# The rows' scales reach all partitions through a small vector in DRAM and a repeating transfer, in place of a product of ones with a diagonal

## The chip, the cores and the metric

The kernel runs on one core of a Trainium2 chip. The metric is the device time of one execution in microseconds (us), here the median of several; lower is better. The engines of the core are named as in the profile: PE is TensorE (matrix products), PEld its loading of weights, DVE is VectorE, ACT ScalarE, POOL GpSimd, and SP is SyncE, which in this kernel issues nearly all transfers between DRAM and the on-chip memory, in the order of its queue. Each engine works through its own queue in order and waits on semaphores for the others.

## The reference

A decoder of two layers over 2048 rows of 1024 features: a gated retention layer (phase A) and a gated sliding-window attention layer (phase B). What matters here is the row scale, the reciprocal root mean square of a row, which multiplies the input of every projection:

```python
def rms(x):
    xf = x.astype(jnp.float32)
    return (xf * lax.rsqrt(jnp.mean(xf * xf, axis=-1, keepdims=True) + EPS)).astype(x.dtype)

def rmsnorm(x, g):
    return (rms(x) * g).astype(x.dtype)

def retention_layer(x, g_norm, w_in, w_out, sin, cos):
    proj = rmsnorm(x, g_norm) @ w_in
    q, k, v, gate = jnp.split(proj, ...)
    ...
    o = rms(retention(q, k, v)) * silu(gate)
    return x + o @ w_out

def swa_layer(x, g_norm, w_in, g_q, sinks, w_out, k_band, v_band, bias, mask):
    proj = rmsnorm(x, g_norm) @ w_in
    ...
    return x + (attention(q, k_band, v_band, bias, sinks) * silu(gate)) @ w_out
```

## The kernel before

The rows are worked on in four groups g of T = 512, with the features on the 128 partitions and the rows along the free axis. Products in float32 accuracy are made of three passes each, since both factors are split into a high and a low part (raw, whi and wlo for weights; ACT makes the high part at L125 and DVE the low part at L126).

Phase A has 16 units u, one for each group g and retention head h. A unit projects q and k (pp_a2qk and so on, with u in the name; the rotation of the result, L580 to L585, frees the PSUM banks), then v and the gate. From unit 4 on, v and the gate (tensors named a6v, a10v) are made by a Strassen scheme with seven products, p = 0 to 6. In parallel runs the retention of the unit before (names ending in _r: S is the state, Shi and Slo its parts, dl its increment, o the output, kt and ot transposes) and its output projection (pp_ao). Phase B has eight units (g, kv) with the attention.

The row scales have to reach all partitions, since the rows lie along the free axis, while the statistics give them as r, a tile of 128 x 4 with row 128 m + p at partition p, column m. This is done at seven places, in two functions, and the same way in both: DVE scales the unit matrix by each column of r, which gives four diagonal blocks (128 x 512); PE multiplies a matrix of ones with it (a float32 product, two passes), so that each of the 128 partitions gets the 512 scales; DVE copies the result from PSUM.

- stage_rows(g), for g = 1, 2, 3, prepares the inputs of the next group in DRAM, during the last units of the group before. Diagonal dgx (L313), product rpx (L315), copy rbx (L317). Then four rounds k follow: two loads xst (L323), their scaling by the gain ags and rbx on DVE (L327), four sums for the Strassen scheme (L331 to L334), two stores xn (L337) and four stores xS (L339). Six buffers (tag st) hold the round's tiles. Its scales r come from row_stats (POOL, L301). I call these three places sites 1, 2 and 3.
- scales(g), for g = 0 to 3, serves phase B. It loads the sums of squares (L169), adds them over the partitions (ssq, L172), makes r on POOL (L175), then the diagonal (L178), the product rp (L180) and the copy rb (L181). r itself is used early by the keys and values; rb is used first by the gates. It is called once at the end of phase A (L819) and by row_scales in phase B.

Both run beside other work. In phase A a list named behind holds such pieces as generators; step() advances the first of them by one yield at fixed points of a unit's projections. The function drive interleaves the projections of one unit with the retention of the one before. In phase B, at(i, ...) puts a call i steps ahead. The order in which the program is written does not set the queues by itself: the kernel is built under TileContext(schedule_with_timeline_sim=True), which orders each engine's queue by a modelled timeline.

## Time and profile before

| | |
|---|---|
| time, median of 3 runs | 2477.26 us (2474.19 to 2480.29) |
| the profiled execution | 2477.26 us, span 2475.5 us |
| granted TensorE clock | 0.993 |
| busy: PE, DVE, ACT, POOL | 98%, 66%, 43%, 9% |
| moved by transfers | 500 MB, 202 GB/s |

The span is what the profile shows of the execution, from its first instruction to its last; 1.76 us of the time lie around it. Starts in the timelines count from the span's start. A group's row gives the busy time, the mean time of one instruction, and how long its engine sat idle just before them; a row of the waits gives total, times and longest.

### The profile page before, as it was taken

The page shows a single profiled execution, that of the slowest core. Times are in us where ns is not written, and L with a number is a line of the kernel's source. Part 1 is how long each engine was busy: PE and PEld are TensorE (multiplying, and loading weights), DVE is VectorE, ACT ScalarE, POOL GpSimd, SP SyncE. Part 2 cuts the span into 40 slices and gives each one's busy share as a digit, 9 for nine tenths or more (in the row PEclk, how much of TensorE's full clock was granted, in tenths as well). Part 3 has the DMA queues.
Part 4 walks back from the last instruction along what each step waited for, and adds up shares of the span by engine and source line. Part 5 has one row for each costly group of instructions (what it writes and reads, how often), then busy time and mean ns, then how long its engine had stood idle before and what let it go on. Part 6 is the DMA issues. An engine that isn't in the chain of part 4 may idle for free.

```text
span 2475.5 us, 32133 instructions
## 1 busy us (share of the span) xinstructions
PE 2418.5 (98%) x11576; PEld 1965.9 (79%) x11576; DVE 1624.1 (66%) x2898; ACT 1055.0 (43%) x2028; POOL 234.6 (9%) x288
## 2 busy tenths in 40 slices
PE   8999999999999999999999999999999999999997
PEld 6888778887878888887788888887687787777776
DVE  5546665787778668588667765744656566566665
ACT  4333233543536455355455543433424334334332
POOL 0000000110001020001002000022101101102010
PEclk9999999999999999999999999999999999999998
DMA  8433843589786477498548843646554674655661
GB/s 297 141 116 128 285 136 115 187 310 322 228 285 218 129 255 265 134 309 296 160 153 292 290 128 94 207 149 220 192 204 147 231 239 136 211 201 184 201 216 69
DMA packets 178075, 499.97 MB, mean 202 GB/s; under 512 B 20363, under 2 KB 32956, under 8 KB 177916
## 3 DMA queue, kind: packets, MB, share of 16 engines
q1 hardware_dynamic: 177836, 497.66, 59.8%
q8 instruction: 91, 1.49, 0.2%
q14 instruction: 68, 0.56, 0.1%
q0 software_dynamic: 80, 0.26, 0.0%
HBM read 396.11 MB, written 104.88 MB: 202 GB/s over the span
## 4 chain that ended last, share of the span: by engine, by line
PE 54%; DVE 4%; DMA 3%; ACT 1%; SPq 0%; issue 0%; POOL 0%; ACTq 0%; DVEq 0%; POOLq 0%
PE o_t L1117 3%; PE pp_ao L146 2%; PE pp_ao L147 2%; PE pp_ao L148 2%; PE s_t L1068 2%; PE pp_bo L256 2%; PE pp_bo L255 2%; PE pp_bo L257 2%; PE pT_t L1099 1%; PE qtp_b L963 1%; DVE P_t L1071 1%; DMA wlo<-in_w_b 1%; PE ot_r L726 0%; PE o_r L698 0%; PE o_r L700 0%; PE o_r L699 0%
## 5 line engine op out<-in xcount | busy, mean ns | idle before, releaser
L146 PE MATMUL pp_ao<-ohi_r,whi_ao 128*128 128x512 f32 x512 | 198.8, 392 | 6.5 <-ACT whi_ao L125 5.5
L147 PE MATMUL pp_ao<-olo_r,whi_ao 128*128 128x512 f32 x512 | 199.6, 390 | 0.0
L148 PE MATMUL pp_ao<-ohi_r,wlo_ao 128*128 128x512 f32 x512 | 194.2, 390 | 0.9 <-DVE wlo_ao L126 0.9
L1071 DVE CUSTOM_DVE_ANT_0 P_t<-s_t,bias,nsnk 128x256 f32<-128x256 f32 (+1 forms) x256 | 115.1, 472 | 89.7 <-PE s_t L1068 80.1
L1081 ACT ACTIVATE P_t<-P_t,nm_t 128x128 f32<-128x128 f32 x256 | 100.4, 394 | 117.2 <-DVE P_t L1078 114.9
L766 DVE TENSOR_TENSOR x_r<-x_r,pp_ao 128x512 f32<-128x512 f32 x128 | 86.4, 683 | 63.7 <-PE pp_ao L148 63.4
L114 POOL TENSOR_SCALAR r_o_r<-sso_r,ep 128x1 f32<-128x1 f32 x48 | 34.8, 725 | 900.9 <-ACT jo_r L720 900.9
L146 PEld LDWEIGHTS pp_ao<-ohi_r,whi_ao 128*128 128x128 f32 x512 | 96.0, 188 | 27.7 <-ACT whi_ao L125 6.7
L795 ACT CAST Shi_r<-S 128x512 fp32r<-128x512 f32 x120 | 69.9, 618 | 112.3 <-PE o_r L700 74.0
L148 PEld LDWEIGHTS pp_ao<-ohi_r,wlo_ao 128*128 128x128 f32 x512 | 96.1, 188 | 21.6 <-DVE wlo_ao L126 1.6
L147 PEld LDWEIGHTS pp_ao<-olo_r,whi_ao 128*128 128x128 f32 x512 | 96.3, 188 | 19.7
L1068 PEld LDWEIGHTS s_t<-kst,qst_b 128*128 128x128 f32 x512 | 81.9, 193 | 30.5 <-DVE nm_t L1071 11.4
L1068 PE MATMUL s_t<-kst,qst_b 128*128 128x256 f32 (+1 forms) x512 | 97.6, 296 | 8.4 <-DVE nm_t L1071 8.2
L125 ACT CAST whi_ao<-raw_ao 128x1024 fp32r<-128x1024 f32 x64 | 67.1, 1049 | 90.0 <-DMA raw_ao<-in_wo_a 21.9
L796 DVE TENSOR_TENSOR Slo_r<-S,Shi_r 128x512 fp32r<-128x512 f32 x120 | 81.0, 704 | 34.0 <-ACT Shi_r L795 33.8
L126 DVE TENSOR_TENSOR wlo_ao<-raw_ao,whi_ao 128x1024 fp32r<-128x1024 f32 x64 | 78.2, 1222 | 33.5 <-ACT whi_ao L125 33.3
L713 DVE SCALAR_TENSOR_TENSOR S<-S,dl_r 128x512 f32<-128x512 f32 x112 | 74.3, 682 | 27.9 <-PE dl_r L692 27.8
L1102 ACT COPY pTs_t<-pT_t 128x512 f32<-128x512 f32 x64 | 37.3, 583 | 121.1 <-PE pT_t L1099 120.8
L256 PE MATMUL pp_bo<-olo_t,whi_bo 128*128 128x512 f32 x224 | 88.3, 394 | 0.0
L257 PE MATMUL pp_bo<-ohi_t,wlo_bo 128*128 128x512 f32 x224 | 88.2, 394 | 0.0
L255 PE MATMUL pp_bo<-ohi_t,whi_bo 128*128 128x512 f32 x224 | 85.5, 397 | 0.5 <-ACT ohi_t L1136 0.5
L964 ACT CAST qst_b<-qtp_b 128x512 fp32r<-128x512 f32 x64 | 37.4, 585 | 84.0 <-PE qtp_b L963 83.9
(1040 smaller groups left out, 7129.5 us busy)
## 6 DMA issues: line engine op xcount, KB each, us to landing
raw_ao<-in_wo_a SPq DMA_DIRECT2D x64, 512.0 KB, 4.1
b<-in_w_vg SPq DMA_DIRECT2D x64, 256.0 KB, 4.8
res<-xmid SPq DMA_DIRECT2D x28, 512.0 KB, 4.4
whi_bo<-wo SPq DMA_DIRECT2D x28, 512.0 KB, 3.9
wlo_bo<-wo SPq DMA_DIRECT2D x28, 512.0 KB, 4.8
x_r<-in_x_t SPq DMA_DIRECT2D x16, 512.0 KB, 6.4
xin<-in_x SPq DMA_DIRECT2D x16, 512.0 KB, 3.6
xmid<-x_r SPq DMA_DIRECT2D x16, 512.0 KB, 4.9
```

Of the source, the lines that this page charges most:

```text
L126: nc.vector.tensor_tensor(lo, raw, hi.bitcast(F32), op=ALU.subtract)
L146: nc.tensor.matmul(o, hi[:, kk, sl], xh, start=st, stop=False)
L147: nc.tensor.matmul(o, hi[:, kk, sl], xl, start=False, stop=False)
L148: nc.tensor.matmul(o, lo[:, kk, sl], xh, start=False, stop=sp)
L255: nc.tensor.matmul(o, hi[:, kk, sl], xh, start=s, stop=False)
L256: nc.tensor.matmul(o, hi[:, kk, sl], xl, start=False, stop=False)
L257: nc.tensor.matmul(o, lo[:, kk, sl], xh, start=False, stop=e)
L766: nc.vector.tensor_tensor(t, t, ps, op=ALU.add)
L796: nc.vector.tensor_tensor(lo, src[:, d, :], hi.bitcast(F32), op=ALU.subtract)
L1068: nc.tensor.matmul(o, q[:, h, :], kst[:, kv * 2 + hl, kb + b0 : kb + 2, :], start=hl == 0, stop=hl == 1)
L1071: nc.vector.tensor_tensor_reduce(out=pt[:, j, :w], in0=o, in1=bias[:, kv * GQ + h, b0 * P :], scale=-1.0, scalar=nsnk[:, kv * GQ + h : kv ...
L1081: nc.scalar.activation(pt[:, i, :P], pt[:, i, :P], AF.Exp, scale=-1.0, bias=nm[:, i : i + 1], accum_out=den[:, i : i + 1])
```

## The change

A new function, spread, writes r to a vector rd of 512 elements in DRAM (a transfer that writes single elements, since r has the rows of a block on the partitions), and returns a function that loads rd into all 128 partitions, 2 KB into each. The two transfers are issued on SP; the second waits for the landing of the first. The diagonals, the products and the copies go. scales becomes a generator: it yields after the load of the sums, after r, between the two transfers and at its end. scales(0) now stands in the list behind during the last but one unit, and row_scales takes its steps by at(1 to 4). stage_rows yields between the two transfers. The diagonal's buffers go as well (tag sta has one in place of two).

```diff
@@ -163,10 +163,16 @@
 
     scaled = {}
 
-    def scales(g, tiles, tag, rb):
-
-        acc, dg = tiles
+    def spread(r, name):
+
+        d = dram.tile([T], F32, name=f"rd_{name}")
+        nc.sync.dma_start(d.rearrange("(m p) -> p m", p=P), r)
+        return lambda rb: nc.sync.dma_start(rb, d.partition_broadcast(P))
+
+    def scales(g, acc, tag, rb):
+
         nc.sync.dma_start(acc, sqs[g])
+        yield
         ps = bank(f"ssq_{g}", tag)
         for m in range(MT):
             nc.tensor.matmul(ps[:, m : m + 1], acc[:, m * P : (m + 1) * P], ones[:, :1], start=True, stop=True)
@@ -174,12 +180,12 @@
         nc.vector.tensor_scalar(eps, ps[:, :MT], 1.0 / D, EPS, op0=ALU.mult, op1=ALU.add)
         nc.gpsimd.tensor_tensor(r, eps, neghalf[:, :MT], op=ALU.pow)
         nc.vector.tensor_scalar_mul(eps, eps, EPS)
-        for m in range(MT):
-            nc.vector.tensor_scalar_mul(dg[:, m * P : (m + 1) * P], ident, r[:, m : m + 1])
-        rp = bank(f"rp_{g}", tag)
-        nc.tensor.matmul(rp, ones, dg, start=True, stop=True)
-        nc.vector.tensor_copy(rb, rp)
         scaled[g] = r, eps, rb
+        yield
+        load = spread(r, f"b{g}")
+        yield
+        load(rb)
+        yield
 
     def out_proj(src, ohi, olo, evac, name):
         pre = []
@@ -308,14 +314,10 @@
             d = st["rows", g] = [dram.tile([P, 2, T], F32, name=f"xn{kp}_{g}") for kp in range(KT // 2)]
             ds = st["rsums", g] = {n: dram.tile([P, KT // 2, H], F32, name=f"x{n}_{g}") for n in SX}
             r = st["stats", g][1]
-            dg = stp(f"dgx_{g}")
-            for m in range(MT):
-                nc.vector.tensor_scalar_mul(dg[:, m * P : (m + 1) * P], ident, r[:, m : m + 1])
-            rp = bank(f"rpx_{g}")
-            nc.tensor.matmul(rp, ones, dg, start=True, stop=True)
+            load = spread(r, f"x{g}")
+            yield
             rb = small.tile([P, T], F32, tag="rb", bufs=1, name=f"rbx_{g}")
-            nc.vector.tensor_copy(rb, rp)
-            yield
+            load(rb)
             for k in range(KT // 2):
                 t = [stp(f"xst_{g}_{k}_{j}") for j in range(2)]
                 for j in range(2):
@@ -810,13 +812,14 @@
             if u + 1 in (8, 9, 10, 12, 13, 14):
                 behind.append(stage_b(todo[:9]))
                 del todo[:9]
+            if u + 1 == nu - 1:
+                behind.append(scales(0, short("acc_0"), "rr", small.tile([P, T], F32, tag="rb", bufs=1, name="rb_0")))
             drive(tc, main(u + 1), ret(u), 2 if u + 1 < PLAIN else 3, 0)
             for _ in itertools.islice(bias, 2 if u >= RH else 0):
                 pass
             if u < nu - 2:
                 for _ in out_a(u):
                     pass
-        scales(0, [short(f"stb_{i}") for i in range(2)], "rr", small.tile([P, T], F32, tag="rb", bufs=1, name="rb_0"))
         rows = load_xb(0)
 
         def beside():
@@ -1033,8 +1036,10 @@
 
         def row_scales(g):
             pool, tag = ((small, "rb"), (p1, "rb1"))[g % 2]
-            scales(g, [p1.tile([P, T], F32, tag="sta", bufs=2, name=f"st{i}_{g}") for i in range(2)], "f",
-                   pool.tile([P, T], F32, tag=tag, bufs=1, name=f"rb_{g}"))
+            work = scales(g, p1.tile([P, T], F32, tag="sta", bufs=1, name=f"acc_{g}"), "f",
+                          pool.tile([P, T], F32, tag=tag, bufs=1, name=f"rb_{g}"))
+            for i in range(4):
+                at(i + 1, next, work)
 
         def rows(g):
```

Line numbers grow by 2 or 3 behind the edit: the scaling is L329 now, the sums L333 to L336, the rotation L582 to L585, and the update of the state S, at L713 before, is L715. The scheduler orders the queues anew. Three places of DVE's queue follow; the numbers at the ends of names are the tiles' own.

DVE at site 1, ahead of the projections of unit 2 (xst_1_0_0: group 1, round 0, first tile; wlo_a2qk_11 is the last piece of the weights for q and k of unit 2). Before:

```order
L313 TENSOR_SCALAR dgx_1_1863<-ident_r_128,rx_1_1577 128x128 x4
L723 SCALAR_TENSOR_TENSOR gate_a1_0_1325<-o_r1_0_1508,r_o_r1_0_1523,gate_a1_0_1325 128x512
L126 TENSOR_TENSOR wlo_a2qk_11_1668<-raw_a2qk_11_1665,whi_a2qk_11_1667 128x1024
L126 TENSOR_TENSOR wlo_a2v_0_1794<-raw_a2v_0_1791,whi_a2v_0_1793 128x1024
L732 TENSOR_TENSOR olo_r1_1470<-ot_r1_0_1527,ohi_r1_1469 128x4x128
L713 SCALAR_TENSOR_TENSOR S32_1_1471<-S32_1_1471,dl_r1_1_0_1610 128x512
L713 SCALAR_TENSOR_TENSOR S32_1_1471<-S32_1_1471,dl_r1_1_1_1614 128x512
L796 TENSOR_TENSOR Slo_r1_1_1638<-S32_1_1471,Shi_r1_1_1637 128x512 x2
L723 SCALAR_TENSOR_TENSOR gate_a1_1_1327<-o_r1_1_1618,r_o_r1_1_1648,gate_a1_1_1327 128x512
L674 SCALAR_TENSOR_TENSOR klo_r1_1_1634<-kt_r1_1_1628,khi_r1_1_1633 128x512
```

And now:

```order
L725 SCALAR_TENSOR_TENSOR gate_a1_0_1325<-o_r1_0_1508,r_o_r1_0_1523,gate_a1_0_1325 128x512
L329 SCALAR_TENSOR_TENSOR xst_1_0_0_1897<-xst_1_0_0_1897,ags_122,rbx_1_1895 128x512
L329 SCALAR_TENSOR_TENSOR xst_1_0_1_1898<-xst_1_0_1_1898,ags_122,rbx_1_1895 128x512
L126 TENSOR_TENSOR wlo_a2qk_11_1668<-raw_a2qk_11_1665,whi_a2qk_11_1667 128x1024
L333 TENSOR_TENSOR xss_1_0_0_1934<-xst_1_0_0_1897,xst_1_0_1_1898 128x256
L335 TENSOR_TENSOR xss_1_0_1_1935<-xst_1_0_0_1897 128x256
L126 TENSOR_TENSOR wlo_a2v_0_1794<-raw_a2v_0_1791,whi_a2v_0_1793 128x1024
L334 TENSOR_TENSOR xss_1_0_0_1934<-xss_1_0_0_1934,xst_1_0_0_1897 128x256
L734 TENSOR_TENSOR olo_r1_1470<-ot_r1_0_1527,ohi_r1_1469 128x4x128
L715 SCALAR_TENSOR_TENSOR S32_1_1471<-S32_1_1471,dl_r1_1_0_1610 128x512
L329 SCALAR_TENSOR_TENSOR xst_1_1_0_1999<-xst_1_1_0_1999,ags_122,rbx_1_1895 128x512
L715 SCALAR_TENSOR_TENSOR S32_1_1471<-S32_1_1471,dl_r1_1_1_1614 128x512
```

In the diagonal's place, but behind the gate, stand the two scalings of round 0, which need the broadcast rbx; the weights' parts for unit 2 come behind them, and the scalings of round 1 stand among the updates of the state and ahead of the next gate. Rounds 2 and 3 follow in the same way, round 2 ahead of the rotation (L582) and round 3 ahead of its last part. Before, the first scaling stood behind all of these. In SP's queue the two transfers stand behind the second load of the weights for v; the stores of round 0 follow them, then the loads of round 1.

DVE at site 2, in the Strassen products p = 5 and 6 of unit 6 (wlo_a6v_60 and _61 are the weights of p = 6). Before:

```order
L313 TENSOR_SCALAR dgx_2_5583<-ident_r_128,rx_2_5445 128x128 x4
L126 TENSOR_TENSOR wlo_a6v_50_5560<-raw_a6v_50_5557,whi_a6v_50_5559 128x1024
L126 TENSOR_TENSOR wlo_a6v_51_5595<-raw_a6v_51_5592,whi_a6v_51_5594 128x1024
L431 TENSOR_TENSOR r_a6v_40_5547<-r_a6v_40_5547,pp_a6vb30_5450 128x512
L431 TENSOR_TENSOR r_a6v_41_5548<-r_a6v_41_5548,pp_a6vb31_5451 128x512
L317 COPY rbx_2_5590<-rpx_2_5588 128x512
L126 TENSOR_TENSOR wlo_a6v_60_5621<-raw_a6v_60_5618,whi_a6v_60_5620 128x1024
L327 SCALAR_TENSOR_TENSOR xst_2_0_0_5614<-xst_2_0_0_5614,ags_122,rbx_2_5590 128x512
L327 SCALAR_TENSOR_TENSOR xst_2_0_1_5615<-xst_2_0_1_5615,ags_122,rbx_2_5590 128x512
L651 TENSOR_TENSOR s_r6_5831<-sc_r6_5822,mask_164 128x512
L331 TENSOR_TENSOR xss_2_0_0_5638<-xst_2_0_0_5614,xst_2_0_1_5615 128x256
```

And now:

```order
L126 TENSOR_TENSOR wlo_a6v_50_5555<-raw_a6v_50_5552,whi_a6v_50_5554 128x1024
L126 TENSOR_TENSOR wlo_a6v_51_5583<-raw_a6v_51_5580,whi_a6v_51_5582 128x1024
L329 SCALAR_TENSOR_TENSOR xst_2_0_0_5604<-xst_2_0_0_5604,ags_122,rbx_2_5602 128x512
L329 SCALAR_TENSOR_TENSOR xst_2_0_1_5605<-xst_2_0_1_5605,ags_122,rbx_2_5602 128x512
L433 TENSOR_TENSOR r_a6v_40_5542<-r_a6v_40_5542,pp_a6vb30_5445 128x512
L433 TENSOR_TENSOR r_a6v_41_5543<-r_a6v_41_5543,pp_a6vb31_5446 128x512
L715 SCALAR_TENSOR_TENSOR S32_6_5470<-S32_6_5470,dl_r6_0_0_5840 128x512
L333 TENSOR_TENSOR xss_2_0_0_5628<-xst_2_0_0_5604,xst_2_0_1_5605 128x256
L335 TENSOR_TENSOR xss_2_0_1_5629<-xst_2_0_0_5604 128x256
L715 SCALAR_TENSOR_TENSOR S32_6_5470<-S32_6_5470,dl_r6_0_1_5844 128x512
L126 TENSOR_TENSOR wlo_a6v_60_5611<-raw_a6v_60_5608,whi_a6v_60_5610 128x1024
L653 TENSOR_TENSOR s_r6_5821<-sc_r6_5812,mask_164 128x512
```

The scalings stand ahead of the last additions (L433) and of wlo_a6v_60, and the updates of the state S, which stood much later, come ahead of it too. In PE's queue the six passes dl of this update, the first three of the output o and, further on, its last three were moved forward with them: the first use of wlo_a6v_60 is ten passes further back in the queue than before, that of wlo_a6v_61 fifteen, the product rpx taken off.

DVE at site 3, ahead of the rotation of unit 10. Before:

```order
L126 TENSOR_TENSOR wlo_a10qk_11_8643<-raw_a10qk_11_8640,whi_a10qk_11_8642 128x1024
L126 TENSOR_TENSOR wlo_a10v_00_8774<-raw_a10v_00_8771,whi_a10v_00_8773 128x1024
L713 SCALAR_TENSOR_TENSOR S32_9_8192<-S32_9_8192,dl_r9_1_0_8674 128x512
L713 SCALAR_TENSOR_TENSOR S32_9_8192<-S32_9_8192,dl_r9_1_1_8678 128x512
L796 TENSOR_TENSOR Slo_r9_1_8702<-S32_9_8192,Shi_r9_1_8701 128x512
L580 TENSOR_TENSOR q_a10_8558<-pp_a10qk_0_8560,cos_a8_6764 128x512
L581 TENSOR_TENSOR th_a10_0_1_8754<-pp_a10qk_0_8560,sin_a8_6765 128x512
L796 TENSOR_TENSOR Slo_r9_1_8702<-S32_9_8192,Shi_r9_1_8701 128x512
L582 TENSOR_TENSOR th_a10_0_0_8753<-pp_a10qk_1_8561,sin_a8_6765 128x512
L583 TENSOR_TENSOR q_a10_8558<-pp_a10qk_1_8561,cos_a8_6764 128x512
```

And now:

```order
L715 SCALAR_TENSOR_TENSOR S32_9_8182<-S32_9_8182,dl_r9_1_0_8664 128x512
L334 TENSOR_TENSOR xss_3_0_0_8907<-xss_3_0_0_8907,xst_3_0_0_8873 128x256
L336 TENSOR_TENSOR xss_3_0_1_8908<-xst_3_0_1_8874,xss_3_0_0_8907 128x256
L329 SCALAR_TENSOR_TENSOR xst_3_1_0_8971<-xst_3_1_0_8971,ags_122,rbx_3_8871 128x512
L329 SCALAR_TENSOR_TENSOR xst_3_1_1_8972<-xst_3_1_1_8972,ags_122,rbx_3_8871 128x512
L333 TENSOR_TENSOR xss_3_1_0_8999<-xst_3_1_0_8971,xst_3_1_1_8972 128x256
L335 TENSOR_TENSOR xss_3_1_1_9000<-xst_3_1_0_8971 128x256
L715 SCALAR_TENSOR_TENSOR S32_9_8182<-S32_9_8182,dl_r9_1_1_8668 128x512
L334 TENSOR_TENSOR xss_3_1_0_8999<-xss_3_1_0_8999,xst_3_1_0_8971 128x256
L336 TENSOR_TENSOR xss_3_1_1_9000<-xst_3_1_1_8972,xss_3_1_0_8999 128x256
L798 TENSOR_TENSOR Slo_r9_1_8692<-S32_9_8182,Shi_r9_1_8691 128x512
L582 TENSOR_TENSOR q_a10_8548<-pp_a10qk_0_8550,cos_a8_6754 128x512
```

Two scalings of round 0 stand just ahead of wlo_a10v_00, out of the rows shown. The sums of round 0, and the scalings and sums of round 1, now stand ahead of the rotation (L582) and among the updates of the state; a scaling of round 2 stands between the rotation's two halves. PE's queue is as before there, without the product.

For the four places of scales, the diagonal and the copy are gone from DVE's queue, and no instruction waits for rb before the gates.

## The prediction

> **What bounds the kernel now.** I read the page first: TensorE's share and the chain that ended last.
>
> ```profile
> span 2475.5 us, 32133 instructions
> PE 2418.5 (98%) x11576; PEld 1965.9 (79%) x11576; DVE 1624.1 (66%) x2898; ACT 1055.0 (43%) x2028; POOL 234.6 (9%) x288
> PE 54%; DVE 4%; DMA 3%; ACT 1%; SPq 0%; issue 0%; POOL 0%; ACTq 0%; DVEq 0%; POOLq 0%
> ```
>
> TensorE (PE) is busy in 98% of the span, so a pass taken from it is time saved, and a microsecond in which it stands is time lost. Next come its waits, longest first, some left out.
>
> ```profile
> PE s_t L1068 <- DVE nm_t L1071: 8.2, 8, 1.3
> PE pT_t L1099 <- DVE P_t L1093: 7.9, 3, 4.0
> ...
> PE pp_b0g L255 <- DMA whi_b0g<-wg: 2.1, 1, 2.1
> ...
> PE pp_ao L148 <- DVE wlo_ao L126: 0.9, 1, 0.9
> ```
>
> They are short, and none is a wait on the broadcast product, its diagonal or the row statistics. The change can therefore gain the product's own passes, and little more, and can lose by any new wait.
>
> **What is removed.** All instructions of the old way, by tile:
>
> ```profile
> L313 DVE TENSOR_SCALAR dgx<-ident_r,rx x12: 274/281/315, 193.8 to 1022.6; 128x128 f32<-128x128 f32 x12
> L315 PE MATMUL rpx<-dgx,ones x6: 590/592/593, 238.0 to 1057.4; 128*128 128x512 f32 x6
> L317 DVE COPY rbx<-rpx x3: 681/682/684, 239.4 to 1059.0; 128x512 f32<-128x512 f32 x3
> L180 PE MATMUL rp<-st,ones x6: 590/590/591, 1740.7 to 2151.0; 128*128 128x512 f32 x6
> L180 PE MATMUL rp<-stb,ones x2: 590/590/591, 1598.4 to 1598.8; 128*128 128x512 f32 x2
> ```
>
> Two passes for each of seven products: 14. Passes overlap, so their durations are not the price. The chain has the occupancy of a pair; of its rows for five pairs, the first and the last:
>
> ```profile
> 1057.15 0.86 PE rpx L315 x2
> ...
> 2150.74 0.86 PE rp L180 x2
> ```
>
> The gain is 7 x 0.86 = 6.0 us, all on TensorE. VectorE (DVE) loses 28 scalings of 0.28 and seven copies of 0.68, 12.6 us, which lie beside TensorE's work and count for nothing unless one of the waits above ends on them. I take nothing.
>
> **What is added.** Two transfers in a row at each of seven places, both on SP: 512 elements written to DRAM, and after they have landed 128 copies of 2 KB read back. The time from the scales r to the broadcast tile is what matters. The trace has no such pair, so I take the nearest rows:
>
> ```profile
> Sd<-S SPq DMA_DIRECT2D x12, 512.0 KB, 3.8
> xst<-in_x_t SPq DMA_DIRECT2D x24, 256.0 KB, 4.6
> ...
> S<-Sd SPq DMA_DIRECT2D x12, 512.0 KB, 4.2
> ...
> bdr<-bd SPq DMA_DIRECT2D x16, 192.0 KB, 6.0
> ...
> stb<-sqs SPq DMA_DIRECT2D x1, 256.0 KB, 3.2
> ags<-in_ag SPq DMA_DIRECT2D x1, 4.0 KB, 1.8
> ...
> rb<-in_relb SPq DMA_DIRECT2D x1, 2.0 KB, 8.0
> ```
>
> Sd and S are the same pattern, a tile written to DRAM and read back: 3.8 + 4.2, plus some 0.4 for the issues, 8.4 us. Small rows go from 1.8 (ags, at the idle start) to 8.0 (rb, 2 KB); a 256 KB read landed in 3.2 at best here, and the broadcast read of DRAM rows took 6.0. So the bounds are 1.8 + 3.2 + 0.4 = 5.4 and 8.0 + 6.0 + 0.4 = 14.4. I take 8.4, since at the three staging places a megabyte or more has just been issued on the same queue, as it has around Sd.
>
> The store writes single elements. The nearest row is the load of the band bias in 2,048 pieces: the instruction behind it on SP took 5.33 us, not the usual 0.3 to 0.4.
>
> ```profile
> 1677.93 5.33 SPq L169 DMA_DIRECT2D st<-sqs  x1
> ```
>
> A quarter of the pieces makes 1.3 us, inside the bounds. The Trainium skill ("DMA: Bandwidth & Descriptors", Rules for kernel authors) speaks against the change here: a non-contiguous last dimension becomes one descriptor per element. If that 1.3 us came on top of 8.4 at the three staging places, the sum below would be 3.9 us higher.
>
> **What is moved.** This decides. In stage_rows the old product stood some 35 us behind r at the sites of groups 1 and 3, and 3.5 us behind at group 2. The scheduler now puts the broadcast and the first scalings directly behind r: in VectorE's queue they stand where the diagonal stood, ahead of work that TensorE needs soon. VectorE works in order, so while it waits for the broadcast all of that waits too. The three r are ready at the ends of these rows: 193.73, 664.54, 1022.01.
>
> ```profile
> 192.69 1.04 POOL L301 TENSOR_TENSOR rx<-ssx,neghalf 128x4 f32<-128x4 f32 x1
> ...
> 663.53 1.01 POOL L301 TENSOR_TENSOR rx<-ssx,neghalf 128x4 f32<-128x4 f32 x1
> ...
> 1021.00 1.01 POOL L301 TENSOR_TENSOR rx<-ssx,neghalf 128x4 f32<-128x4 f32 x1
> ```
>
> Site 1, what VectorE delivers and when TensorE takes it (the scaling of a pair from site 2):
>
> ```profile
> 196.69 1.23 DVE L126 TENSOR_TENSOR wlo_a2qk<-raw_a2qk,whi_a2qk 128x1024 fp32r<-128x1024 f32 x1 [1.21 <-ACT whi_a2qk L125]
> ...
> 674.00 1.41 DVE L327 SCALAR_TENSOR_TENSOR xst<-xst,ags,rbx 128x512 f32<-128x512 f32 x2
> ...
> 202.40 0.39 PE L571 MATMUL pp_a2qk<-xhi_a,wlo_a2qk 128*128 128x512 f32 x1
> ...
> 216.06 0.39 PE L150 MATMUL pp_a2v<-whi_a2v,xhi_a 128*128 128x512 f32 x1
> ```
>
> Broadcast at 193.7 + 8.4 = 202.1, the pair 1.4, then wlo_a2qk 1.2: 204.7, against 202.4 wanted: 2.3 us. Then the rounds: SP issues round k+1's loads only behind the stores of round k, which wait for its scalings, and they land 4.6 us later. Round 1's loads land at about 209, round 2's second at 218.2, and round 2's pair stands ahead of the rotation that frees the first bank for pp_a2v. With two sums and two rotations it is free at 220.7, against 216.06 + 2.3 = 218.4: 2.3 more. The last bank, behind a scaling of round 3, costs about 0.8. Site 1: 5.4.
>
> Site 2:
>
> ```profile
> 672.87 1.22 DVE L126 TENSOR_TENSOR wlo_a6v<-raw_a6v,whi_a6v 128x1024 fp32r<-128x1024 f32 x1
> ...
> 676.30 0.39 PE L451 MATMUL pp_a6vb<-whi_a6v,xhi_a 128*128 128x512 f32 x1
> 676.53 0.39 PE L452 MATMUL pp_a6vb<-wlo_a6v,xhi_a 128*128 128x512 f32 x1
> ...
> 679.73 0.48 PE L452 MATMUL pp_a6vb<-wlo_a6v,xhi_a 128*128 128x512 f32 x1
> ```
>
> Broadcast at 672.9, the pair to 674.3, four additions of 0.6, two sums of 0.33 and wlo_a6v 1.1 behind it: 678.5. Here TensorE's queue moved as well: ten passes of the state update and the output now stand ahead of this use and fifteen ahead of the next. At 0.23 a pass, less the 0.45 more that the removed pair held, the uses come at 678.4 and 682.7. The first loses 0.1. Nine instructions on, 5.6 us, the next wlo_a6v ends at 684.1: 1.4 lost. Together 1.5, and the 0.9 us that TensorE now waits for wlo_ao right behind (at 683) goes into it.
>
> Site 3:
>
> ```profile
> 1036.48 0.68 DVE L580 TENSOR_TENSOR q_a<-pp_a10qk,cos_a 128x512 f32<-128x512 f32 x1
> ...
> 1038.90 0.39 PE L451 MATMUL pp_a10va<-whi_a10v,xhi_a 128*128 128x512 f32 x1
> ...
> 1040.29 0.62 PE L451 MATMUL pp_a10va<-whi_a10v,xhi_a 128*128 128x512 f32 x2
> ```
>
> Broadcast at 1030.4, pair to 1031.8, stores and round 1's loads issued to 1033.0, landed 1037.6. Both pairs now stand ahead of the rotation that began at 1036.48. Pair, sums, state and rotations end at 1042.4 against 1038.90: 3.5 us. The second bank, behind a scaling of round 2, is free at 1046.0 against 1040.29 + 3.5: 2.2. Site 3: 5.7.
>
> The other four sites (scales) have no such wait: r is split off, and its broadcast is first used in the gates, many microseconds on. But SP stands for the store, about 4 us, and the loads behind it start late. They run ahead as far as buffers let them; SP mostly waits for TensorE:
>
> ```profile
> SPq L237 <- PE pp_bo L257: 102.0, 18, 22.9
> ```
>
> The store's landing is the 3.8 of above. I take 0.5 in all for the four sites, from nothing to 4 x 3.8 = 15 if that lead were gone.
>
> Sum: -6.0 - 0.9 + 5.4 + 1.5 + 5.7 + 0.5 = +6.2 us. The profiled execution took 2477.26, 1.76 above its span, and is the median of the three runs: 2483.5. A microsecond of landing more counts three times, once at each staging site; one less counts twice, since site 2 has only 1.5 to give.
>
> **The rivals.** What a measurement of this kernel can tell from no change is about 0.3%, 7.4 us.
>
> A, the forecast: VectorE waits for the broadcast, above all at sites 1 and 3, and gives back what TensorE gains and a little more: 2483.5, inside that bound.
>
> B, quick landing: at 5.4 us sites 1 and 3 give 3.0 each and site 2 its 1.5, and the sum is -1.3: 2476.0, no change. For it: 3.2 us for stb. Against it: the medians above, 3.8 and more where the queue is filled. The Trainium skill gives a rule that leads here ("DMA: Bandwidth & Descriptors", Anatomy of one DMA): about 2.0 us fixed for a transfer plus its bytes at 436 GB/s. By it the two take an estimated 2.0 + 2.6 us, 5.0 with the issues, which makes 2475.2; the rows above are mostly longer than it gives.
>
> C, covered: TensorE has other slack around the sites that I have missed, the stalls come to nothing, and VectorE's 12.6 us shorten some of the 16 us of attention waits by up to 4: from 2470.4 down to 2466.4. For it: TensorE's list of waits has none at sites 1 and 3 now. Against it: the slack counted above is shorter than the landing.
>
> D, the other side: a slow broadcast. 128 partitions read the same 2 KB of DRAM, as bdr's load reads the same rows 128 times, and take that row's 6.0 us. The landing is then 3.8 + 6.0 + 0.4 = 10.2, 1.8 more, three times: +5.4, 2488.9, slower. It decides from a landing of 8.8 on. For it: bdr moves less and took longer than S. Against it: bdr is written to DRAM, the broadcast to the partitions.
>
> E: SP's queue. Weights of the second phase come late at four sites, up to 15 us: 2498. It decides once a load's lead is under the store's 4 us. For it: the single wait on whi_b0g, 2.1. Against it: the 102 us for which SP waits for TensorE to free buffers.
>
> **How the numbers follow.** A 0.40, B 0.22, C 0.16, D 0.17, E 0.05. My replay of the queues can be off by 4 us either way, so of A a third lies beyond +7.4. Faster by over 0.3% takes most of C and a little of B: 0.14. Within 0.3%: two thirds of A, most of B, the rest of C: 0.50. Slower: the rest of A, D and E: 0.36. The range goes from 2468 (inside C) to 2495 (between D and E); the forecast's own runs from 2479 to 2488.
>
> **What would show it.** In the profile after: 14 passes and 28 scalings gone; landing from r to rbx of 8.4 us; VectorE's scaling (L329 now) waiting for the broadcast by 2 to 8 us at each of three sites; TensorE waiting for wlo_a2qk, wlo_a6v and for rotations in front of pp_a2v and pp_a10va, 12 to 13 us together; in the second phase no new wait for weights. A landing under 6 us, or TensorE without waits at these sites, would make it wrong.

## The result: 18 us slower, and the profile after

The kernel before took 2478.36 us (median of 6 runs, 2473.42 to 2484.93), the changed one 2496.78 (6 runs, 2492.43 to 2502.38): a ratio of 1.0077, with an interval of 1.0061 to 1.0092. That is slower by more than the 0.3% that can be told from no change, and 13 us over the forecast. The profiled execution took 2495.08. First the page of the changed kernel: span, busy times, and the chain that ended last by engine.

```profile
span 2493.1 us, 32083 instructions
PE 2415.9 (97%) x11562; PEld 1967.0 (79%) x11562; DVE 1612.9 (65%) x2863; ACT 1054.5 (42%) x2028; POOL 239.3 (10%) x288
PE 50%; DMA 6%; DVE 5%; ACT 1%; issue 1%; SPq 0%; POOL 0%; ACTq 0%; DVEq 0%; POOLq 0%
```

The 14 passes are gone (11,576 to 11,562), TensorE is busy for 2.6 us less, and yet the span is 17.6 us longer: TensorE stands. In the chain, transfers went from 3% to 6%. The 14 passes alone would have made it 6.0 less; where the other 3.4 of busy time come from is told below. The waits of TensorE in the changed kernel (in all, times, longest, us; some left out):

```profile
PE s_t L1073 <- DVE nm_t L1076: 12.7, 14, 2.0
...
PE pp_a10va L453 <- ACT khi_r L675: 8.0, 1, 8.0
...
PE pp_a2qk L573 <- DVE wlo_a2qk L126: 6.6, 1, 6.6
PE pp_a6vb L453 <- DVE r_a6v L433: 5.5, 1, 5.5
...
PE pp_a6vb L454 <- DVE wlo_a6v L126: 2.2, 1, 2.2
...
PE pp_a10va L453 <- ACT r_a10v L462: 2.0, 1, 2.0
...
PE pp_a2v L150 <- DVE th_a L583: 1.2, 1, 1.2
...
PE pp_a10va L453 <- DVE q_a L585: 0.4, 1, 0.4
```

Units 2, 6 and 10 (pp_a2, pp_a6, pp_a10) are the three staging sites. Their new waits are 6.6 + 1.2 = 7.8 at site 1, 5.5 + 2.2 = 7.7 at site 2 and 8.0 + 2.0 + 0.4 = 10.4 at site 3: 25.9 us. The 5.5 in front of pp_a6vb is a wait that the forecast did not name: for the last additions (L433) of the product before, which stand behind the scalings like wlo_a6v. What stands in front of all of them is the landing. The scales r end in POOL's timeline at 193.78, 671.04 and 1034.48:

```profile
192.74 1.04 POOL L307 TENSOR_TENSOR rx<-ssx,neghalf 128x4 f32<-128x4 f32 x1
...
670.03 1.01 POOL L307 TENSOR_TENSOR rx<-ssx,neghalf 128x4 f32<-128x4 f32 x1
...
1033.47 1.01 POOL L307 TENSOR_TENSOR rx<-ssx,neghalf 128x4 f32<-128x4 f32 x1
```

SP issues the store (L169) at once, and the broadcast (L170) as soon as the store has landed, 8.8, 10.0 and 8.5 us later:

```profile
193.80 0.38 SPq L169 DMA_DIRECT2D rd_x<-rx  x1
...
202.59 0.33 SPq L170 DMA_DIRECT2D rbx<-rd_x  x1
...
671.07 0.38 SPq L169 DMA_DIRECT2D rd_x<-rx  x1
...
681.09 0.32 SPq L170 DMA_DIRECT2D rbx<-rd_x  x1
...
1034.51 0.38 SPq L169 DMA_DIRECT2D rd_x<-rx  x1
...
1042.97 0.33 SPq L170 DMA_DIRECT2D rbx<-rd_x  x1
```

VectorE's first scaling then starts at 207.07, 687.31 and 1047.62. In its timeline the time in brackets is what it stood idle just before:

```profile
207.07 1.42 DVE L329 SCALAR_TENSOR_TENSOR xst<-xst,ags,rbx 128x512 f32<-128x512 f32 x2 [11.61 <-DMA rbx<-rd_x]
208.40 1.22 DVE L126 TENSOR_TENSOR wlo_a2qk<-raw_a2qk,whi_a2qk 128x1024 fp32r<-128x1024 f32 x1
...
687.31 1.42 DVE L329 SCALAR_TENSOR_TENSOR xst<-xst,ags,rbx 128x512 f32<-128x512 f32 x2 [10.54 <-DMA raw_ao<-in_wo_a]
...
1047.62 1.41 DVE L329 SCALAR_TENSOR_TENSOR xst<-xst,ags,rbx 128x512 f32<-128x512 f32 x2 [9.91 <-DMA rbx<-rd_x]
...
1058.07 0.68 DVE L582 TENSOR_TENSOR q_a<-pp_a10qk,cos_a 128x512 f32<-128x512 f32 x1
1058.67 0.68 DVE L583 TENSOR_TENSOR th_a<-pp_a10qk,sin_a 128x512 f32<-128x512 f32 x1
```

From r to the scaling it is 13.3, 16.3 and 13.1 us, where 8.4 was forecast. Right behind the scaling at site 1 comes wlo_a2qk, which ends at 209.62, and TensorE's 6.6 us end there: the stall goes through VectorE's order as the forecast has it. Two releasers have to be read with care. At 687.31 the profile names raw_ao, but the broadcast had been issued at 681.09 and the scaling needs it. The 8.0 us in front of pp_a10va are put down to ScalarE's khi_r, but they end when the first bank is free again, after the rotation (L582 and L583) at 1059.3.

The transfers by issue to landing; the last figure of each row is the median:

```profile
rb<-rd_b SPq DMA_DIRECT2D x4, 256.0 KB, 5.5
rbx<-rd_x SPq DMA_DIRECT2D x3, 256.0 KB, 4.6
...
rd_b<-rbx SPq DMA_DIRECT2D x4, 2.0 KB, 9.4
rd_x<-rx SPq DMA_DIRECT2D x3, 2.0 KB, 9.2
```

The store of 2 KB takes twice as long as the read of 256 KB behind it. Most of that is not time in which data move. Windows from about 3 us behind the store's issue to the issue of the broadcast, at sites 1 and 3 (length, then the busy times of PE, PEld, DVE, ACT and POOL with their instructions, the granted clock, the busy share of the transfer engines and GB/s):

```profile
197.20:202.50 5.30, 5.30 (x27) 4.38 (x26) 0.00 (x0) 1.64 (x2) 0.00 (x0) 1.00 0.02 3
1037.60:1042.90 5.30, 5.30 (x26) 4.37 (x24) 0.12 (x1) 0.00 (x0) 0.00 (x0) 1.00 0.00 0
```

For the last 5.3 us the transfers of the core carry 3 and 0 GB/s, so nothing stands in the queue ahead of the store there; SP waits for its completion alone.

The stalls cost more than their length. Behind each of them the passes run slowly, in these windows from the stall's end (at site 2 with the second wait of 2.2 inside):

```profile
209.60:212.90 3.30, 3.23 (x8) 2.57 (x9) 3.30 (x8) 0.00 (x0) 0.00 (x0) 0.56 0.81 200
689.40:697.40 8.00, 5.72 (x13) 4.12 (x14) 8.00 (x15) 5.90 (x9) 0.00 (x0) 0.51 0.86 261
1059.40:1063.10 3.70, 3.24 (x8) 2.19 (x8) 2.60 (x5) 0.96 (x2) 0.00 (x0) 0.59 0.75 237
```

The granted clock is 0.56, 0.51 and 0.59 there, against 1.00 in the windows above, and a pass of this size starts 0.43 us after the one before in place of 0.23. At 0.23 a pass these 29 would take 6.7 us, and they take 12.2: 5.5 us more, which the forecast had not counted.

Not everything that moved was a loss. Two windows hold units 3 and 11, from one unit's first product for q and k to the next one's. Before:

```profile
289.70:400.90 111.20, 107.16 (x490) 87.79 (x488) 70.85 (x91) 41.78 (x57) 4.75 (x8) 1.00 0.51 166
1113.60:1228.00 114.40, 110.09 (x494) 89.93 (x493) 86.32 (x111) 60.99 (x90) 11.30 (x12) 0.97 0.72 238
```

After:

```profile
300.60:405.30 104.70, 104.70 (x482) 86.93 (x481) 63.45 (x78) 41.52 (x55) 4.52 (x8) 1.00 0.41 131
1138.40:1244.50 106.10, 105.66 (x490) 87.48 (x489) 80.61 (x103) 55.95 (x80) 8.59 (x10) 1.00 0.64 211
```

TensorE stood 111.20 - 107.16 = 4.0 and 114.40 - 110.09 = 4.3 us in these units before, and 0.0 and 0.4 after: 7.9 us of waits are gone that the forecast had not looked at. In unit 11 the passes were slow as well (clock 0.97): taking 0.23 us for each of the four passes fewer, its busy time is 3.5 us shorter. VectorE has 13 and 8 instructions fewer there. In unit 3 eight of them are sums for Strassen weights (b, from stage_sums), which stand behind stage_rows in the list behind. Of their four rows by line the last, with its first and last start, before:

```profile
L374 DVE TENSOR_TENSOR b<-b,b x4: 681/684/692, 279.4 to 308.6; 128x512 f32<-128x512 f32 x4
```

After:

```profile
L376 DVE TENSOR_TENSOR b<-b,b x4: 691/692/692, 252.1 to 282.1; 128x512 f32<-128x512 f32 x4
```

Before, they reach 19 us into unit 3, which begins at 289.7; after, they end 18 us ahead of it (300.6). The first scaling of group 1 moved from 240.6 to 207.1, and what stands behind it in the list moved with it. In unit 11 it is the pieces of stage_b: 12 splits on VectorE before, 7 after.

In the second phase only the last group of scales costs something. SP stands for its store from 2172.14 to 2181.63:

```profile
2172.14 1.31 SPq L169 DMA_DIRECT2D rd_b<-rbx  x1
...
2181.63 0.32 SPq L170 DMA_DIRECT2D rb<-rd_b  x1
```

The loads of x for the next unit wait behind it, and that stretch, from unit b5's first product to b6's, is 4.5 us longer than before (111.6 against 107.1). TensorE's waits in it are 5.5 in place of 1.6; 4.2 are for VectorE in the attention (s_t) and 1.3 for a part of x (xhi_b). That the late loads are behind the 4.2 is not followed further. Together: -6.0 for the passes, -0.9 for wlo_ao, -7.9 in units 3 and 11, +25.9 at the sites and +4.5 here make +15.6 of 17.6; with the slow passes, +5.5 at the sites and -3.5 in unit 11, it is 17.6. So close a fit is in part luck: stretches of a hundred microseconds vary by some 3 us from one kernel's profile to another's with nothing changed in them.

### The profile page after: what moved, and what is told of

The parts are those of the page before. It is cut to its first block, busy times and chain, and to the rows that moved or that the text cites. A ratio compares the mean times of both kernels' runs of the same rounds, so it can differ in the third digit from the quotient of the medians.

```text
span 2493.1 us, 32083 instructions
## 1 busy us (share of the span) xinstructions
PE 2415.9 (97%) x11562; PEld 1967.0 (79%) x11562; DVE 1612.9 (65%) x2863; ACT 1054.5 (42%) x2028; POOL 239.3 (10%) x288
## 2 busy tenths in 40 slices
DMA packets 182779, 501.82 MB, mean 201 GB/s; under 512 B 24171, under 2 KB 36764, under 8 KB 182620
## 4 chain that ended last, share of the span: by engine, by line
PE 50%; DMA 6%; DVE 5%; ACT 1%; issue 1%; SPq 0%; POOL 0%; ACTq 0%; DVEq 0%; POOLq 0%
PE o_t L1122 2%; PE pp_ao L146 2%; PE pp_ao L147 2%; PE pp_ao L148 2%; PE s_t L1073 2%; PE pp_bo L262 2%; PE pp_bo L263 2%; PE pp_bo L261 2%; PE pT_t L1104 1%; DMA xraw<-xmid 1%; DVE P_t L1076 1%; PE qtp_b L966 1%; DMA wlo<-in_w_b 1%; DMA Sd<-S 0%; PE o_r L700 0%
## 5 line engine op out<-in xcount | busy, mean ns | idle before, releaser
L1073 PE MATMUL s_t<-kst,qst_b 128*128 128x256 f32 (+1 forms) x512 | 97.7, 296 | 12.7 <-DVE nm_t L1076 12.7
L715 DVE SCALAR_TENSOR_TENSOR S<-S,dl_r 128x512 f32<-128x512 f32 x112 | 74.1, 679 | 21.8 <-PE dl_r L694 21.6
L725 DVE SCALAR_TENSOR_TENSOR gate_a<-o_r,r_o_r,gate_a 128x512 f32<-128x512 f32 x64 | 47.8, 747 | 38.4 <-POOL r_o_r L115 36.4
```

The lines of the kernel that those rows point to most:

```text
L1073: nc.tensor.matmul(o, q[:, h, :], kst[:, kv * 2 + hl, kb + b0 : kb + 2, :], start=hl == 0, stop=hl == 1)
```

## The experiments

The theory when the first four were made: the mechanism of the forecast holds, and its landing was too short, because the store of 4-byte pieces takes 9 us. Rivals: the four scales places cost the time by SP's queue; or the new order of VectorE costs it, whatever the landing. Each ratio is against the kernel before on the same chip.

**One part alone.** The first run keeps the product in stage_rows and changes only scales.

```diff
-            load = spread(r, f"x{g}")
-            yield
+            dg = stp(f"dgx_{g}")
+            ...
+            nc.tensor.matmul(rp, ones, dg, start=True, stop=True)
...
-            load(rb)
+            nc.vector.tensor_copy(rb, rp)
```

> Only the four places of scales go through DRAM; the three staging places multiply as before. Theory 1 (VectorE's scalings stand in front of what TensorE needs and wait for a landing of some 13 us at the three staging places): the loss goes away, and four pairs of passes, 3.4 us, are gained, less what SP's standing behind the element store costs in the second phase (4 us seen around the last group): 2475 to 2480. Rival 2 (the blocked SP queue, wherever the broadcast stands, makes weights late): most of the loss stays, 2488 or more.

Measured: 2479.51 against 2477.84, 1.0008 [0.9996, 1.0019]: no change. SP's own waits have this row:

```profile
SPq L170 <- DMA rd_b<-rbx: 36.4, 4, 9.7
```

SP stands 36 us in all, and TensorE sees little of it. The four pairs' 3.4 us and the last group's stretch (3.6 us longer here) about cancel.

The second run is the other half: scales by the product, stage_rows through DRAM.

```diff
-    def scales(g, acc, tag, rb):
+    def scales(g, tiles, tag, rb):
...
+        rp = bank(f"rp_{g}", tag)
+        nc.tensor.matmul(rp, ones, dg, start=True, stop=True)
+        nc.vector.tensor_copy(rb, rp)
...
-        load = spread(r, f"b{g}")
-        yield
-        load(rb)
```

> Only the three staging places go through DRAM; scales multiplies as before. Theory 1: nearly the whole loss, 2492 to 2496. Rival 2: three sevenths of it, about 2486.

Measured: 2489.26 against 2477.84, 1.0050 [1.0030, 1.0069]: a miss by 2.7 us, and about as near to the number of rival 2. What decides between the two is the run before, where rival 2 gave 2488 or more and 2479.51 came, and the profile here: TensorE's waits at the three sites are 21.5 us. The loss is in the staging; the two halves, 0.08% and 0.50%, add up to 0.58% of the whole's 0.77%, inside the intervals.

**The size of the landing.** This run has every instruction of the changed kernel in the same order on TensorE and VectorE. The store writes each partition's four values side by side, 128 pieces of 16 bytes, so the scales come in another order than the rows.

```diff
-        nc.sync.dma_start(d.rearrange("(m p) -> p m", p=P), r)
+        nc.sync.dma_start(d.rearrange("(p m) -> p m", p=P), r)
```

> The changed kernel with one edit: the vector is stored in 128 pieces of 16 bytes, not in 512 single elements, so that the scales come back in another order (the result's rows are scaled wrongly). The order of the work on VectorE and TensorE stays the same to the row. Theory 1, with the element store as the term that was mis-sized: the store lands in about 4 us, VectorE waits some 5 us less at each staging place, and the time is what was forecast for a landing of 8.4 us, 2480 to 2487. Rival 3 (the landing is set by the queue ahead of it or by the write to DRAM, not by the number of pieces): the store still takes 8 to 9 us, 2495 to 2499. Rival 4 (the new order of the work costs by itself): time unchanged though the landing is shorter.

Measured: 2479.38 against 2477.84, 1.0007 [0.9992, 1.0022]. Its transfers:

```profile
rbx<-rd_x SPq DMA_DIRECT2D x3, 256.0 KB, 3.7
...
rd_x<-rx SPq DMA_DIRECT2D x3, 2.0 KB, 4.4
```

The store fell from 9.2 to 4.4. From r to the first scaling it is now 6.4, 9.0 and 7.4 us, and VectorE's wait for the broadcast is 10.1 us in all three sites, where it was 11.61 + 10.54 + 9.91 = 32.1:

```profile
DVE xst L329 <- DMA rbx<-rd_x: 10.1, 3, 4.7
```

TensorE's waits at the three sites fall from 25.9 to 8.7. With nothing else changed the loss is gone, so the store's landing is what costs (the read behind it is a little shorter too, 3.7 for 4.6). The new order alone is not dear.

**No transfer at all.** All seven places take a copy on GpSimd in place of the two transfers. Every partition repeats its own first scale, so the spreading over the partitions is left out.

```diff
-        d = dram.tile([T], F32, name=f"rd_{name}")
-        nc.sync.dma_start(d.rearrange("(m p) -> p m", p=P), r)
-        return lambda rb: nc.sync.dma_start(rb, d.partition_broadcast(P))
+        return lambda rb: nc.gpsimd.tensor_copy(rb, r[:, 0:1].to_broadcast([P, T]))
```

> The changed kernel with a copy by GpSimd in place of the two transfers: all partitions' rows get the first column of r, which leaves out the spreading over the partitions (wrong scales). The scalings stand as early in VectorE's queue as in the changed kernel, or earlier. Theory 1: without a landing nothing waits, 14 passes are gone, 2468 to 2473. Rival 4 (the early place of the staging rounds costs by itself, since each round's loads stand behind the stores of the round before): 2480 or more.

Measured: 2464.36 against 2477.84, 0.9951 [0.9936, 0.9966], 13.5 us faster, where the passes are worth 6.0. So the order of the changed kernel is better than the old one once the landing is short, by more than the forecast had counted. The last run below takes this up.

**16-byte pieces with the right order.** Can the changed kernel have the short store? In e5 the rows of x for the statistics of groups 1 to 3 are read so that partition p holds the rows 4p to 4p + 3; then the 16-byte pieces are in order at the staging places. The scales of the second phase keep single elements.

```diff
-                nc.sync.dma_start(xin, x[(g * MT + m) * P : (g * MT + m + 1) * P, :])
+                rows = x[g * T : (g + 1) * T, :].rearrange("(p m) d -> m p d", m=MT)[m] if g else x[m * P : (m + 1) * P, :]
+                nc.sync.dma_start(xin, rows)
...
-            load = spread(r, f"x{g}")
+            load = spread(r, f"x{g}", "(p m) -> p m")
```

> The changed kernel with the store repaired at the staging places: the rows of groups 1 to 3 are read as row 4 p + m at partition p, so that 128 pieces of 16 bytes come back in the right order. The four stores of scales keep their 512 elements. Theory 1: the staging places cost what they cost with 16-byte pieces everywhere, and the second phase what it cost with the elements (about 4 us around the last group): 2480 to 2485. Rival 3 (the landing isn't set by the number of pieces): 2495 or more.

Measured: 2482.41 against 2478.38, 1.0018 [1.0008, 1.0028]. Both kinds of store stand in one profile:

```profile
rd_b<-rbx SPq DMA_DIRECT2D x4, 2.0 KB, 9.9
rd_x<-rx SPq DMA_DIRECT2D x3, 2.0 KB, 3.5
```

**The product, earlier.** If an early start of the staging is worth something, the kernel before should gain by it too: here its product is written right behind the row statistics, with no transfer.

```diff
+                    if g:
+                        row_product(g, r)
...
-            load = spread(r, f"x{g}")
+            rb = st.pop(("rbx", g))
```

> The kernel before, with the product of the staging places written directly behind the row statistics, two steps earlier: at group 1 it then stands 111 passes further ahead in TensorE's queue, and the rounds start some 25 us earlier. All 14 passes stay. Theory 5 (what the copy on the chip gained beyond the 6 us of the passes came from the early rounds, which take VectorE's crowding out of units 3 and 11, where TensorE waited 4 us each): 2469 to 2474. Rival 6 (it came from the removed VectorE work, 12.6 us): no change, 2476 to 2479.

Measured: 2479.18 against 2478.38, 1.0004 [0.9992, 1.0017]: a miss. The first scaling comes at 226.1, not directly behind r at 193.8, since the product waits for its turn in TensorE's queue. The time is what rival 6 gave, at its upper end. The profile, of the slowest of the 12 runs (2484.83), divides them: unit 3 became 4.8 us shorter (106.4) with all of VectorE's work kept, as theory 5 has it; unit 11 was 119.7 long. So the gain at one place was lost at another. The next run, with the same staging, has 106.5 and 117.8. Why unit 11 is worse is open, and with it whether rival 6 holds there.

**The same with the short store at scales.** The staging has the product of e6; the scales go through DRAM. The sums are taken a second time over every fourth column, so that the 16-byte pieces are in order there too.

```diff
+            nc.tensor.matmul(ps[:, MT + m : MT + m + 1], acc[:, m::MT], ones[:, :1], start=True, stop=True)
...
-        load = spread(r, f"b{g}")
+        load = spread(r[:, MT:], f"b{g}")
```

> The early product for the three staging places, and scales through DRAM in 16-byte pieces, for which the sums of squares are added a second time in row order 4 p + m (four one-column products more). Theory 1 and 5 together: SP stands 3 us and not 10 at each of the four places, four pairs of passes less, 3.4 us: 2466 to 2471, below the kernel before. Rival 2 (the blocked SP queue): as the early product alone or slower.

Measured: 2486.9 against 2478.38, 1.0043 [1.0027, 1.0058]: a miss. The products over the strided columns (L179) are dearer than expected (shortest, median and longest ns of one):

```profile
L178 PEld LDWEIGHTS ssq<-ones,acc x32: 188/189/208, 1537.3 to 2165.2; 128*128 128x128 f32 x32
...
L179 PEld LDWEIGHTS ssq<-ones,acc x32: 308/320/332, 1537.7 to 2165.5; 128*128 128x128 f32 x32
L179 PE MATMUL ssq<-ones,acc x32: 280/370/373, 1537.7 to 2165.6; 128*128 128x1 f32 x32
```

A weight load of every fourth column takes 320 ns where one of neighbouring columns takes 189, and the product behind it 370. The products overlap, so these durations are not the price. At the first place the 16 products hold TensorE for 2.66 us (1537.56 to 1540.22), where the eight of e1 hold it for 0.81; the others are alike, and four such places make 7.4 us. The forecast also counted on e6's gain, which did not come: 2479.18 of e6, less 3.4, plus 7.4 is 2483.2. The 3.7 beyond that are open.

**Number or size of the pieces?** The store again in 512 pieces, as in the changed kernel, but of 16 bytes each (every value four times); only the first 2 KB are read back, so the rows get other scales than their own.

```diff
+        r4 = small.tile([P, MT, MT], F32, tag="r4", bufs=1, name=f"r4_{name}")
+        nc.gpsimd.tensor_copy(r4, r.unsqueeze(2).to_broadcast([P, MT, MT]))
+        nc.sync.dma_start(d.rearrange("(m p e) -> p m e", p=P, e=MT), r4)
```

> The changed kernel with r copied four times by GpSimd and stored as 512 pieces of 16 bytes, of which the first 2 KB are read back (wrong scales). If the number of pieces sets the landing: 9 to 10 us for the store, 2495 to 2499. If the 4 bytes of a piece set it: 3 to 4.5 us, 2478 to 2483.

Measured: 2488.68 against 2478.38, 1.0045 [1.0030, 1.0061]. The store:

```profile
rd_x<-r_x SPq DMA_DIRECT2D x3, 8.0 KB, 4.3
```

As many pieces with four times the bytes land in less than half the time. The packets that the profile counts bear the edit out: 182,780 here and 182,779 in the changed kernel, 180,091 in e3, where seven stores have 384 pieces fewer. So it is the size of the piece, 4 bytes, and not the number. The time as a whole was a miss: VectorE's wait for the broadcast is about as short as in e3 (12.4 us at all three sites), and the 10 us lie elsewhere, against the kernel before about 4 us in units 4 and 5 and about 5 between unit 12 and the second phase's third. TensorE's passes themselves are slower there. Unit 12 in e8, then in e3:

```profile
1232.80:1326.70 93.90, 93.90 (x425) 77.35 (x424) 62.85 (x76) 44.03 (x63) 9.75 (x9) 1.00 0.52 166
...
1230.90:1323.90 93.00, 93.00 (x425) 77.35 (x424) 62.65 (x76) 44.00 (x62) 9.51 (x9) 1.00 0.52 169
```

The same 425 passes, with no idle time and a clock of 1.00 in both, take 0.9 us longer, and other units without waits do so too. It is not a wait for the broadcast; what slows the passes is open.

**The broadcast a unit ahead.** Row statistics and both transfers stand one unit earlier, so that the broadcast is there long before the scalings.

```diff
+            if h == 1 and g + 1 < NG:
+                behind.insert(0, row_stats(g + 1))
...
-                behind.append(row_stats(g + 1))
```

> The changed kernel with the row statistics and both transfers of the staging places a unit earlier, the store of 512 elements kept; the scalings follow when the broadcast has long landed. Theory 1: the landing of 13 us costs nothing where nothing waits for it, 14 passes are gone, and the second phase pays about 4 us around the last group: 2468 to 2474. Rival 7 (the staging rounds, moved earlier, crowd another stretch): no faster than the kernel before.

Measured: 2519.33 against 2479.39, 1.0163 [1.0149, 1.0177], a clear miss. VectorE has no wait for the broadcast any more, but TensorE waits for other things, in units 1, 5 and 9 above all:

```profile
PE ot_r L730 <- DVE gate_a L727: 13.9, 4, 6.2
...
PE pp_a5va L455 <- ACT whi_a5v L125: 4.6, 1, 4.6
PE pp_a9vb L455 <- ACT whi_a9v L125: 4.6, 1, 4.6
```

By windows these waits are 12.5 us in unit 1, 12.3 in unit 5 and 9.2 in unit 9. The row statistics of the next group and its two transfers now lie around these units. That they crowd the engines there is read from these rows and not tested by itself. Unit 2 begins 16 us later than before, unit 6 33 us, unit 10 46 us, of which some comes back. The store landed in 12.3 us by the median here. VectorE no longer stands for it, but SP still does, between store and broadcast (539.9 to 551.3 in unit 5), and a load of weights behind it in the queue (raw_a5v) is issued only at 557.4; the 4.6 us for whi_a5v end at 564.2. So the landing may still cost something here; no run divides it from the rest. The same with the scales by the product:

```diff
-        load = spread(r, f"b{g}")
-        yield
-        load(rb)
+        rp = bank(f"rp_{g}", tag)
+        nc.tensor.matmul(rp, ones, dg, start=True, stop=True)
```

> As the one above at the staging places, and scales multiplies as before, so that SP never stands in the second phase. Theory 1: three pairs of passes less, 2.6 us, the waits of units 3 and 11 that the early rounds relieve, up to 8 us, and no blocked SP: 2467 to 2475. Rival 7: no faster than the kernel before.

Measured: 2518.39 against 2479.39, 1.0154 [1.0133, 1.0176]: the same miss.

**The best of both.** Row order and 16-byte pieces at the staging places (as in e5), the product at the scales (as in e2).

```diff
-        nc.sync.dma_start(d.rearrange("(m p) -> p m", p=P), r)
+        nc.sync.dma_start(d.rearrange("(p m) -> p m", p=P), r)
...
+        rp = bank(f"rp_{g}", tag)
+        nc.tensor.matmul(rp, ones, dg, start=True, stop=True)
```

> The staging places through DRAM with 128 pieces of 16 bytes in row order, scales by the product as before: the row-order kernel without its four places in the second phase. Theory 1: three pairs of passes gained, 2.6 us, waits for a landing of 6 to 9 us at three places lost, SP free in the second phase: 2477 to 2482, no change to the kernel before. Rival 2: SP's standing at the staging places costs too, 2484 or more.

Measured: 2476.95 against 2478.76, 0.9990 [0.9981, 1.0000]. It is the best version that computes all of the reference, and cannot be told from the kernel before.

**The copy on the chip at the staging places alone**, scales by the product; the spreading is left out as in e4.

```diff
-        return lambda rb: nc.sync.dma_start(rb, d.partition_broadcast(P))
+        return lambda rb: nc.gpsimd.tensor_copy(rb, r[:, 0:1].to_broadcast([P, T]))
...
+        rp = bank(f"rp_{g}", tag)
+        nc.tensor.matmul(rp, ones, dg, start=True, stop=True)
```

> The copy on the chip at the three staging places alone (wrong scales there, the spreading over the partitions left out), scales by the product. If the gain of the copy at all seven places (13.5 us) beyond the 6 us of the passes came from the staging rounds, which start at once and no longer crowd units 3 and 11: 2465 to 2469, about 10 us below the kernel before. If it came from the second phase: 2474 or more.

Measured: 2467.10 against 2478.76, 0.9958 [0.9945, 0.9970]. The copy takes 0.61 us, and units 3 and 11 by windows, as above, are:

```profile
288.00:394.20 106.20, 106.20 (x490) 88.13 (x489) 64.67 (x80) 42.44 (x57) 5.18 (x8) 1.00 0.41 131
1106.20:1212.90 106.70, 106.29 (x494) 87.99 (x493) 81.08 (x104) 56.62 (x83) 9.95 (x12) 1.00 0.63 205
```

Idle time is 0.0 and 0.4, as in the changed kernel. With the same number of passes as before the two units are 5.0 and 7.7 us shorter, 12.7 together: 7.9 of idle time, and most of the rest passes that run at a clock of 1.00 in unit 11 in place of 0.97. The two profiles differ by 12.9 in all, the medians by 11.7; what the three pairs gain in other units, 2.6, is lost again elsewhere, within what profiles differ by. The two units are short in every profile with the scalings directly behind r (the changed kernel, e2 to e5, e8, e11, e12): 105 to 106 us and 106 to 108, against 111 and 114 before and 115 and 112 in e1, which stages as before. That the early list of background work is the cause is argued from this, from the rows of b and from these windows. VectorE's removed instructions stood in units 2, 6 and 10, not in 3 and 11, which speaks against rival 6 of e6; e6 itself bears the cause out for unit 3 alone, so for unit 11 it is not shown.

## Why the prediction was wrong

- **The passes, 6.0:** e4 and e12 do not speak against it: without transfers the kernel gains that and more. No run takes the passes away and nothing else.
- **The mechanism:** right in the main. The scalings wait in VectorE's queue at three places, TensorE waits behind them for wlo_a2qk, wlo_a6v and rotations, as forecast, and the scales' transfers make no wait for weights. The largest wait at site 2, 5.5 us for the additions of unit 6 (L433), was not among those named. By e1 and e2 the loss is in the staging, as the sum has it. e3 tests the slope: its landings of 6.4, 9.0 and 7.4 give 3.4 + 2.1 + 4.7 = 10.2 us of stalls by the forecast, and its waits at the sites are 8.7.
- **The step that failed:** "I take 8.4", the landing. I chose the tiles Sd and S, full-width transfers, as the nearest rows. The store of single elements took 9.2 by the median in place of 3.8; the broadcast read took 4.6, near the 4.2 taken. From r to the scaling it came to 13.1 and 13.3, just under the upper bound of 14.4, and at site 2 to 16.3, above it. The nearest row by time, rb with 2 KB in 8.0, would have come closer only by luck: it is a load of 32 rows of 64 bytes, and no row that I had listed has pieces of 4 bytes. With my slope of one for one at each site, 4.9 + 7.9 + 4.7 = 17.5 us more landing makes stalls of 12.6 + 17.5 = 30; 25.9 were measured, and 5.5 more in slow passes behind them, a term that I did not have. e3, which shortens the store alone, takes the loss away.
- **A reading:** at group 1 the old product stood 44 us behind r (193.73 to 238.0), not some 35; the sum does not use it.
- **The sentence on the pieces:** the bias load's row, and with it the rule of the Trainium skill ("DMA: Bandwidth & Descriptors", Rules for kernel authors: one descriptor per element), pointed the right way, and I priced the pieces by the row at 1.3 us a place, 3.9 in all. The sum with it, 2487.4, was still 9 short. Pricing by number was the error: by e8 512 pieces of 16 bytes land in 4.3.
- **The 12.6 us of VectorE's work, "I take nothing", with 0.9 for old waits:** mis-sized the other way. 7.9 us of waits in units 3 and 11 went as well, and 3.5 us of slow passes with them. By e6 the gain in unit 3 comes with the early staging alone, with that work kept. I had looked for waits at the sites of the change, not in the units behind them, where the staging pushes later work of the same list.
- **The four scales places, 0.5:** 4.5 measured at the last group, inside the bounds of 0 to 15; e1 shows that the pairs there pay for it.
- **The rivals:** B fell with the landing. The rule beside it (the Trainium skill, "DMA: Bandwidth & Descriptors", Anatomy of one DMA), by which the store is an estimated 2.0 us, does not agree with the traces: 9.2 with 4-byte pieces, and 3.5 to 4.4 with 16-byte ones. The Trainium skill fits that rule there to transfers issued from GpSimd; these are issued on SP. D had the right direction and the right point (a landing over 8.8), but named the wrong transfer: the broadcast was quick, the store slow. E did not come, apart from the last group. C's claim of other slack was wrong at the sites; with no landing at all the gain is larger than the 10.9 that C gave at most (13.5 in e4, 11.7 in e12), and not by the attention's waits.

The range ended at 2495 because I took its upper end from D and E. The landing's own upper bound, 14.4, was worked out but not carried through: three times 14.4 - 8.4 = 6.0 makes 2483.5 + 18 = 2501.5. That bound belonged in the range.

## What to carry to other kernels

Price a small transfer by rows with pieces of the same size, not by rows with the same purpose; where the profile has no such row, as here, carry the upper bound through to the range. Add the write and the read of a trip through DRAM: here the write of 2 KB in 4-byte pieces cost twice the read of 256 KB. Then look where the first reader of the result stands in its engine's queue, and what stands behind it; a short wait on an engine that works in order is paid by whoever comes next. Earlier is not better in itself: e9 takes the wait away, and is 40 us slower, with new waits in other places.

## What the runs showed of the hardware

- A store of 512 elements of 4 bytes landed in 9.2 to 10.0 us by the medians of most of these kernels, and in 12.3 and 12.9 at the staging places of e9 and e10; 512 pieces of 16 bytes in 4.3, 128 pieces of 16 bytes in 3.5 to 4.4 at the staging places. With 4 bytes the last 5.3 us pass with hardly any transfer under way (0.02 and 0.00 of the engines' time at sites 1 and 3), so more than half of the landing there passes after the transfers have gone quiet. Why it takes so long the runs do not say.
- Behind stalls of TensorE of 5.5 to 8.0 us the granted clock was 0.51 to 0.59 in the windows above, and a pass started 0.43 us after the one before in place of 0.23.
- A weight load of every fourth column of a fp32 tile took 320 ns, of neighbouring columns 189 (e7).
- That SP stood 36 us for stores in the second phase (e1) cost TensorE about 4, around the last group.
